# One core, a whole transformer block: the planner charges for a change of TensorE's tiling, PSUM tiles are taken one at a time, and the last expert's second layer goes by column halves

## The chip, the cores and the metric

One core of a Trainium2 chip runs the whole program. The metric is the device time of one execution in microseconds (us), the median of the runs shown.

## What is computed

The input is 256 tokens of width 1024 in float32. Four parts follow one another, each added to the residual `x`:

- **Layer 1**: a norm, one projection of 4896 columns, a forgetting attention (8 heads), a sparse attention (8 heads, three branches), sigmoid gates, and an output projection `w_out`.
- **Mixture of experts**: a norm, a router that gives each token two of 16 experts, and for each expert `silu(t @ w_gate) * (t @ w_up)`, weighted, times `w_down` (1024 to 512 to 1024). 

```python
hid = jax.nn.silu(jnp.einsum('td,edf->etf', t, w_gate)) * jnp.einsum('td,edf->etf', t, w_up)
hid = hid * combine.T.astype(hid.dtype)[:, :, None]
y = jnp.einsum('etf,efd->td', hid, w_down)
```

- **Two hybrid layers**: a norm, a projection to `q, f, i(v), z` of a gated linear recurrence (8 heads of 128) and `q, k, v, z` of a windowed attention (16 heads of 64), and an output projection `w_out_2` of 2048 rows, normed before it is added.

All weights are read from HBM once, some 200 MB.

## The kernel before

**One program order from a planner.** Nothing is ordered by the hardware or by hand. The kernel is written as tasks (Python generators) that yield one operation at a time, and `Sched.run` plays them against a model of the engines: it holds a clock for each engine, gives each yielded operation a ready time, and on the engine that can go first picks the ready task of the lowest priority number (`P_EDGE` -1, `P_SPLIT` 0, `P_EVAC` 1, `P_SIDE` 2, `P_LATE` 3, `P_MAIN` 9). The order picked is the order of the instruction streams. A task can also wait for a flag, for another task, or for a free buffer (`Res`). Every instruction is recorded at line 216 (`go`), so the profile's rows are told apart by tile names.

**Main products and side products.** The tasks of `P_MAIN` issue the large products: weights against activations. Float32 is carried as a high and a low part in fp32r (`hh` and `hl`, halves `w`), three products for one (`mm3`). The weights arrive as 1 MB pieces (`raw`, tasks of `loader`). For layer 1 and the hybrids each piece is split by ScalarE and VectorE into two halves `w` (`K.half_max` limits how many halves are held); the experts' pieces are used as they are ("whole", "pair"). `K.raw_max` limits the pieces held, and `K.slots` (23 buffers) is shared by pieces, halves and activations.

The side tasks (attention, recurrence, evacuations, transposes) put small products between the main ones. Three tilings of TensorE's array occur: full (128 rows by 128 columns), by columns (128x64: the experts' products, the recurrence's `bank<-ha`, attention's second products `bank<-ap,kv`), and by rows (64x128: attention's scores `bank<-kv,qaT`). Two products of a split tiling that lie on different halves run side by side. A plain float32 product shows as two records.

**The experts.** For expert `e` the main task issues the gate and up products (32 records, `bank<-raw,xt`) and then the second layer of the expert before it, `down(e-1)` (16 records, `bank<-raw,route`). Beside it run `rows_of(e)` (transposes and small products that make the placing matrix `P2` and the weights `ws`), `hidden(e)` (ScalarE and VectorE make silu and product, then two transposes to `hT`) and `combine(e)` (scale the result `py`, split it into a high part on 64 partitions and the low part on the other 64, and four products that add it to the PSUM tiles `acc`). All of these are in the full tiling. Before the second expert group, `halves` splits `x` into `xh` and `xl`. After the last expert the edge to the next layer runs: residual, norm, transposes, `hh` and `hl`.

**PSUM.** Four tiles `acc` (`acc_tile`) hold main results, four `bank`s side results. `out_proj` takes four `acc` tiles and then goes over groups of input columns; a group starts when its heads are done. The hybrid's projections go in a written order that ends with `za3`, `z3`; the first group of `out_proj` needs heads 0 and 1, the second heads 2 and 3, the last two the attention pairs.

`keep_warm` puts products of ones (`warm<-ones`) where the planner sees TensorE idle.

Of the kernel before, what the change touches and what calls it, by code (L numbers as in the profile page):

```python
# [82 lines left out]
class Op:  # L83

    __slots__ = ("alts", "ins", "outs", "half", "ready", "banks", "rows")

    def __init__(self, alts, ins, outs, half=(0, 2)):
        self.alts, self.ins, self.outs, self.half, self.ready = alts, ins, outs, half, None
        self.banks = ()

# [41 lines left out]
class Sched:  # L132
# [4 lines left out]
    def __init__(self, nc):  # L137
        self.clk = {"PE": 600.0, "DVE": 600.0, "ACT": 1900.0, "POOL": 600.0, "SP": 600.0}
        self.dma = 0.0
        self.cols = [0.0, 0.0]  # L140
        self.readers = {}
        self.work, self.cold = [], True
        self.fill = self.halfway = None
        self.slot = {}
        self.acc = {}
        self.tasks, self.n = [], 0
        self.made = self.sent = 0
        self.nc = _NC(self, nc)
# [29 lines left out]
    def op(self, eng, op, f, a, k):  # L178
# [43 lines left out]
        if eng == "PE":  # L222
            o.rows = ins[0].shape[0] / 128 * min(1.0, n / 0.6 / cost if op == "matmul" and ins[-1].dtype == F32 else 1.0)
        else:
            o.banks = {self.slot.get(x.tensor.name, x.tensor.name) for x in aps if str(x.space) == "PSUM"}
# [45 lines left out]
    def _product(self, o, start, cost):  # L271
        lo, hi = o.half
        start = max(start, self.clk["PE"])

# [6 lines left out]
        end = max(start + 53, other) if beside else start + cost  # L281
# [49 lines left out]
    def run(self):  # L331
        while self.tasks:
# [16 lines left out]
            for eng, c in self.clk.items():  # L349
                pick = None  # L350
                for t in self.tasks:
                    if t.pend is None:
                        continue
                    for alt in t.pend.alts:
                        if alt[0] == eng:
# [7 lines left out]
                            key = (late, r if late else 0.0, -1 if t is self.halfway and eng == "PE" else t.prio, t.seq)  # L363
# [48 lines left out]
TO_PE, IDLE = 200.0, 150.0  # L412
HOLD = 200
# [4 lines left out]
def setup(ctx, tc, I):  # L418
# [21 lines left out]
    K.slots, K.tinies = Res(SLOTS), Res(TINY)  # L440
    K.raws, K.raw_max, K.halves, K.half_max = 0, 3, 0, 4
# [46 lines left out]

class Unit:
# [22 lines left out]
def loader(K, between):  # L512
# [5 lines left out]
    def load():  # L518
        yield ("if", lambda: K.go)
        for i, u in enumerate(K.plan):  # L520
            yield ("if", lambda: K.raws < K.raw_max and K.slots.free)
            K.raws += 1
            raw, s = yield from big(K, [128, 2048], "raw")
# [11 lines left out]
    def part(u, i, j, src, sh, w, s):  # L535
# [5 lines left out]
        if all(f.done for f in u.flag):  # L541
            K.raws -= 1
            K.slots.release(raws.pop(i)[1])

    sch.spawn(load(), P_SPLIT)
    for i, u in enumerate(K.plan):
        yield wait(loaded[i])
        if u.how in ("whole", "pair"):
# [129 lines left out]
def out_proj(K, key, groups, done, last=1):  # L678
# [3 lines left out]
    ps = []  # L682
    for i in range(4):
        p = yield from acc_tile(K, [128, 512])
        ps.append(p)
# [3 lines left out]
    def go(g, c, j, t):  # L689
        oh, ol = groups[g][1]()  # L690
# [651 lines left out]
def moe(K, edge, done, before):  # L1342
# [105 lines left out]

    class Group:
# [10 lines left out]
    def rows_of(e):  # L1460

        yield wait(t_w, t_rows.get(e - 1), ys.get(e - 2))
        for t in range(2):
            yield nc.vector.tensor_scalar(dup[:, t].rearrange("p (i s) -> p i s", i=2),
                                          K.c("slot")[:, None, :].to_broadcast([128, 2, CAP]), posm[:, t, e:e + 1], None, op0=OP.is_equal)
        p2, b_ = yield from bank(K, [128, 258])
# [10 lines left out]
    def halves():  # L1477
# [3 lines left out]
        for t in range(2):  # L1481
            yield from split(K, *(a[0][:, t].rearrange("p (k d) -> p k d", k=8) for a in xhl), K.x[:, t].rearrange("p (d k) -> p k d", k=8))
# [46 lines left out]
    def hidden(e, pg, b_):  # L1529
# [6 lines left out]
        K.banks.release(b_)  # L1536
        ph, b_ = yield from bank(K, [128, 2, 128])
# [8 lines left out]
    def combine(e, py, b_):  # L1546
# [8 lines left out]
        yield wait([sp(part(c), P_EVAC if e < NE - 1 else P_EDGE) for c in range(2)])  # L1555
        K.banks.release(b_)
        for t in range(2):
            for c in range(2):
                yield nc.tensor.matmul(acc[2 * t + c][0], P2[:, e % 2, t], ty[:, c], start=(e == 0), stop=(e == NE - 1))
                if e == NE - 1:  # L1560
                    done(t, c, acc[2 * t + c])

    hid = {}

    def down(e):
# [10 lines left out]
        ys[e] = sp(combine(e, py, b_), P_EVAC if e < NE - 1 else P_EDGE)  # L1576
# [12 lines left out]
    for e in range(NE):  # L1589
# [4 lines left out]
        t_rows[e] = sp(rows_of(e), P_SIDE)  # L1594
        pg, b_ = yield from bank(K, [128, 2, 256])
        for u_ in range(4):
# [9 lines left out]
            drop_whole(K, u)  # L1606
        if j == 3:
# [3 lines left out]
        hid[e] = sp(hidden(e, pg, b_), P_EVAC)  # L1611
# [26 lines left out]
    yield from down(NE - 1)  # L1638
    yield wait(ys[NE - 1])
# [630 lines left out]
```

## Time and profile before

| | us |
|---|---|
| median of three runs (lowest, highest) | 1006.81 (1002.85, 1007.44) |
| the profiled execution: time, span | 1005.22, 1003.4 |
| TensorE busy, weight loads busy | 975.9, 748.5 |
| VectorE busy, ScalarE busy | 701.4, 496.7 |
| mean granted TensorE clock | 0.996 of full |

The span is from the first to the last instruction; what lies around it is 1.8 us. Matmuls are pipelined, so one that lasts 0.28 us may be followed by the next after 0.12: the step from start to start is the pace. Stages in the span: layer 1 to 250, experts from 250 to 500, the hybrids from 500 to 745 and from 745 on.

### The profile page before, as it was taken

Reading aid. Unit: us, or ns where it says so; the run is one execution under the profiler, and the core shown is the slowest. Engines: PE = TensorE matmul, PEld = TensorE weight load, DVE = VectorE, ACT = ScalarE, POOL = GpSimd, SP = SyncE. Lnnn points to the kernel's source line nnn. Section 1 sums busy time; section 2 is a strip of 40 time slices with the busy share of each in tenths; the row PEclk is TensorE's granted clock in tenths of the full one; section 3 lists DMA queues with packets and bytes.
Section 4 is the critical chain, followed back from the end, with each engine's and each line's share of the span. In section 5 each row is a group of like instructions: output and inputs, shape, how many; then the busy total and the mean of one; then the engine's idle time right before and its main releaser. Section 6 shows DMA issues by size and latency. Waiting matters only on the chain.

```text
span 1003.4 us, 16635 instructions
## 1 busy us (share of the span) xinstructions
PE 975.9 (97%) x6335; PEld 748.5 (75%) x6335; DVE 701.4 (70%) x1755; ACT 496.7 (50%) x1054; POOL 23.2 (2%) x64
## 2 busy tenths in 40 slices
PE   7999999999999999999899999999999999999998
PEld 6877898897434343434588979888888897988887
DVE  5777888685364444545656898999768489899942
ACT  5556679741121111114335658668664365866841
POOL 0101000000000000000000000000000000000000
PEclk9999999999999999999999999999999999999999
DMA  8822593797899999989910224433936232442321
GB/s 299 293 81 85 170 318 113 266 378 269 302 390 388 407 409 409 409 343 391 363 63 1 84 84 128 130 104 120 336 122 218 67 103 86 130 146 102 125 107 42
DMA packets 106578, 210.33 MB, mean 210 GB/s; under 512 B 6174, under 2 KB 54544, under 8 KB 106496
## 3 DMA queue, kind: packets, MB, share of 16 engines
q1 hardware_dynamic: 105248, 206.00, 57.3%
q0 software_dynamic: 1248, 3.22, 1.0%
q8 instruction: 52, 0.85, 0.4%
q14 instruction: 30, 0.25, 0.1%
HBM read 208.16 MB, written 1.05 MB: 208 GB/s over the span
## 4 chain that ended last, share of the span: by engine, by line
PE 46%; DVE 8%; ACT 1%; issue 1%; DVEq 0%
PE acc L216 32%; PE bank L216 12%; DVE ha L216 3%; DVE w L216 2%; PE warm L216 1%; DVE ap L216 1%; ACT ha L216 1%; DVE hb L216 1%; DVE hn L216 0%; DVE rows L216 0%; DVE tiny L216 0%; DVE x L216 0%; DVE og L216 0%; DVE za L216 0%; ACT w L216 0%
## 5 line engine op out<-in xcount | busy, mean ns | idle before, releaser
L216 DVE TENSOR_TENSOR w<-raw,w 128x1024 fp32r<-128x1024 f32 (+1 forms) x196 | 233.2, 1211 | 28.5 <-ACT w L216 27.4
L216 PE MATMUL acc<-hh,w 128*128 128x256 f32 x1280 | 247.4, 289 | 0.0
L216 ACT ACTIVATE w<-raw 128x1024 fp32r<-128x1024 f32 (+1 forms) x196 | 198.7, 1040 | 46.7 <-PE acc L216 26.4
L216 PEld LDWEIGHTS acc<-hh,w 128*128 128x128 f32 x1280 | 202.9, 192 | 6.2 <-issue 4.1
L216 PE MATMUL acc<-hl,w 128*128 128x256 f32 x640 | 184.8, 289 | 0.0
L216 PE MATMUL acc<-w,hh 128*128 128x512 f32 (+2 forms) x512 | 155.5, 380 | 0.2
L216 PEld LDWEIGHTS acc<-hl,w 128*128 128x128 f32 x640 | 122.6, 192 | 2.3 <-issue 0.7
L216 PE MATMUL bank<-raw,xt 128*64 128x512 f32 x512 | 118.1, 599 | 1.2 <-DVE xt L216 1.2
L216 PEld LDWEIGHTS acc<-w,hh 128*128 128x128 f32 x512 | 92.6, 188 | 17.3 <-issue 2.2
L216 PE MATMUL acc<-w,hl 128*128 128x512 f32 (+2 forms) x256 | 96.6, 377 | 0.0
L216 PE MATMUL acc<-w,og 128*128 128x512 f32 x384 | 88.7, 390 | 0.0
L216 PEld LDWEIGHTS acc<-w,og 128*128 128x128 f32 x384 | 71.9, 188 | 14.8
L216 ACT ACTIVATE route<-bank,route 128x256 f32<-128x256 f32 x16 | 7.6, 473 | 144.9 <-PE bank L216 144.9
L216 PEld LDWEIGHTS bank<-raw,xt 128*64 128x64 f32 x512 | 33.6, 136 | 58.5 <-issue 53.0
L216 DVE TENSOR_TENSOR ha<-ha 128x128 f32<-128x128 f32 (+5 forms) x216 | 69.3, 352 | 0.6
L216 ACT ACTIVATE ap<-ap,tiny 128x256 f32<-128x256 f32 (+1 forms) x98 | 42.9, 448 | 49.0 <-DVE tiny L216 36.5
L216 PE MATMUL bank<-raw,route 128*64 128x512 f32 x256 | 60.3, 604 | 0.0
L216 PEld LDWEIGHTS acc<-w,hl 128*128 128x128 f32 x256 | 48.3, 189 | 8.2 <-issue 1.0
L216 PE MATMUL warm<-ones 128*128 128x256 f32 x275 | 40.1, 297 | 4.6 <-ACT ones L437 2.4
L216 PEld LDWEIGHTS warm<-ones 128*128 128x128 f32 x275 | 36.3, 198 | 8.1 <-ACT ones L437 2.4
L216 PEld LDWEIGHTS bank<-raw,route 128*64 128x64 f32 x256 | 17.4, 138 | 31.8 <-issue 29.5
L216 PE MATMUL bank<-ha 128*64 128x96 f32 (+2 forms) x608 | 37.9, 246 | 0.0
(276 smaller groups left out, 1330.3 us busy)
## 6 DMA issues: line engine op xcount, KB each, us to landing
raw<-in_w_in_dram SPq DMA_DIRECT2D x68, 1024.0 KB, 7.5
raw<-in_w_gate_dram SPq DMA_DIRECT2D x64, 512.0 KB, 8.9
raw<-in_w_up_dram SPq DMA_DIRECT2D x64, 512.0 KB, 9.9
raw<-in_w_down_dram SPq DMA_DIRECT2D x32, 1024.0 KB, 11.5
raw<-in_w_out_dram SPq DMA_DIRECT2D x20, 1024.0 KB, 5.2
raw<-in_cmp_k_w_dram SPq DMA_DIRECT2D x2, 1024.0 KB, 5.7
raw<-in_cmp_v_w_dram SPq DMA_DIRECT2D x2, 1024.0 KB, 5.8
raw<-in_w_fox_up_dram SPq DMA_DIRECT2D x2, 1024.0 KB, 12.2
```

What stands on the lines that cost most here:

```text
L216: go = lambda: f(*a, **k)
```

## The change

- **The planner** gets a tiling for each product (`o.mode`) and adds `SWITCH` (95 ns) when it changes. A side product of another tiling than the current one, of priority between `P_EDGE` and `P_MAIN`, is put behind the main products until `GATHER` (1500 ns) after it became ready. Two halves side by side are modelled 2 ns apart, not 53.
- **Experts**: flags `gate[e]`, set when the gate and up products of `e` are issued. `hidden(e)` transposes after `gate[e+1]`, `combine(e)` multiplies after `gate[e+2]`, `rows_of(e)` uses TensorE after `gate[e]`: all three now fall between gate and up of one expert and `down` of the one before. The tasks of the last two experts get `P_EDGE`.
- **The last `down`** becomes `down_last`: all products of columns 0 to 511, then of 512 to 1023; the two array halves hold two partial sums, which are scaled, split and added by eight products instead of four, the first column half while the second is multiplied.
- **`out_proj`** takes an `acc` tile when its first product comes.
- **`loader`** holds at most four pieces that are yet to be split (`K.parts`).
- **`halves`** splits `x` in eight steps instead of two.

```diff
@@ Sched.op
+            o.mode = (ins[0].shape[0] <= 64, aps[0].shape[0] <= 64) if op == "matmul" and ins[-1].dtype == F32 else (False, False)
@@ Sched._product
+        if o.mode != self.mode:
+            self.mode = o.mode
+            start += SWITCH
+            self.clk["PE"] = start
+            self.cols = [max(c, start) for c in self.cols]
-        end = max(start + 53, other) if beside else start + cost
+        end = max(start + 2, other) if beside else start + cost
@@ Sched.run
-                            key = (late, r if late else 0.0, -1 if t is self.halfway and eng == "PE" else t.prio, t.seq)
+                            prio = -1 if t is self.halfway and eng == "PE" else t.prio
+                            if eng == "PE" and t.pend.mode != self.mode and P_EDGE < t.prio < P_MAIN and r < t.pend.ready + GATHER:
+                                prio = P_MAIN + 0.1
+                            key = (late, r if late else 0.0, prio, t.seq)
+SWITCH, GATHER = 95.0, 1500.0
@@ loader
-            yield ("if", lambda: K.raws < K.raw_max and K.slots.free)
+            whole_ = u.how in WHOLE
+            yield ("if", lambda: K.raws < K.raw_max and K.slots.free and (whole_ or K.parts < 4))
             K.raws += 1
+            K.parts += not whole_
@@ out_proj
-    ps = []
-    for i in range(4):
-        p = yield from acc_tile(K, [128, 512])
-        ps.append(p)
+    ps = {}
     def go(g, c, j, t):
+        if 2 * t + c not in ps:
+            ps[2 * t + c] = yield from acc_tile(K, [128, 512])
@@ rows_of
-        yield wait(t_w, t_rows.get(e - 1), ys.get(e - 2))
+        yield wait(t_w, t_rows.get(e - 1))
...
+        yield wait(gate[e] if e else None, ys.get(e - 2))
         p2, b_ = yield from bank(K, [128, 258])
@@ halves
-            yield from split(K, *(a[0][:, t].rearrange("p (k d) -> p k d", k=8) for a in xhl), K.x[:, t].rearrange("p (d k) -> p k d", k=8))
+            for k in range(0, 8, 2):
+                yield from split(K, *(a[0][:, t].rearrange("p (k d) -> p k d", k=8)[:, k:k + 2] for a in xhl),
+                                 K.x[:, t].rearrange("p (d k) -> p k d", k=8)[:, k:k + 2])
@@ hidden
+        yield wait(gate[e + 1] if e < NE - 1 else None)
         ph, b_ = yield from bank(K, [128, 2, 128])
@@ combine
-        yield wait([sp(part(c), P_EVAC if e < NE - 1 else P_EDGE) for c in range(2)])
+        yield wait([sp(part(c), P_EVAC if e < NE - 2 else P_EDGE) for c in range(2)])
         K.banks.release(b_)
+        yield wait(gate[e + 2] if e < NE - 2 else None)
@@ new
+    def combine_last(c, py, b_, ty2):
+        e = NE - 1
+        yield wait(ys.get(e - 1), t_rows[e])
+        w = ws[:, 0, e:e + 1]
+        yield nc.scalar.activation(ty2[:, c, 0], py, AF.Copy, scale=w)
+        yield nc.vector.scalar_tensor_tensor(ty2[:, c, 1], py, w, ty2[:, c, 0].bitcast(F32), op0=OP.mult, op1=OP.subtract)
+        K.banks.release(b_)
+        for i in range(2):
+            for t in range(2):
+                yield nc.tensor.matmul(acc[2 * t + c][0], P2[:, e % 2, t], ty2[:, c, i], start=False, stop=(i == 1))
+                if i:
+                    done(t, c, acc[2 * t + c])
+    def down_last():
...
+        for c in range(2):
+            py, b_ = yield from bank(K, [128, 512])
+            for h, u in enumerate(us):
+                w = yield from whole(K, u)
+                for b in range(2):
+                    yield nc.tensor.matmul(py[64 * b:64 * b + 64], hT[:, e % 2, b, 64 * h:64 * h + 64], w[:, b, 512 * c:512 * c + 512],
+                                           start=(h == 0), stop=(h == 1))
+            cs.append(sp(combine_last(c, py, b_, ty2), P_EDGE))
@@ moe
-        t_rows[e] = sp(rows_of(e), P_SIDE)
+        t_rows[e] = sp(rows_of(e), P_SIDE if e < NE - 2 else P_EDGE)
+        gate[e].done = True
-        hid[e] = sp(hidden(e, pg, b_), P_EVAC)
+        hid[e] = sp(hidden(e, pg, b_), P_EVAC if e < NE - 2 else P_EDGE)
-    yield from down(NE - 1)
-    yield wait(ys[NE - 1])
+    yield from down_last()
```

## Rows read from the trace of the kernel before

**Rows 1.** Stretches: us; PE, PEld, DVE, ACT, POOL busy; clock; DMA share; GB/s.
```profile
555.00:696.70 141.70, 140.00 (x1217) 124.57 (x1217) 130.44 (x362) 95.85 (x198) 3.21 (x7) 1.00 0.33 105
...
480.00:483.40 3.40, 3.40 (x8) 1.10 (x7) 0.29 (x1) 0.00 (x0) 0.00 (x0) 0.50 1.08 363
```

**Rows 2.** PE's timeline, a hybrid: start, us, tiles, array rows*columns, records, [idle <-releaser].
```profile
569.66 0.40 PE L216 MATMUL acc<-hh,w 128*128 128x256 f32 x2
569.99 0.88 PE L216 MATMUL bank<-ha 128*64 128x96 f32 x16
570.80 0.39 PE L216 MATMUL acc<-hl,w 128*128 128x256 f32 x1
571.03 0.40 PE L216 MATMUL acc<-hh,w 128*128 128x256 f32 x2
```

**Rows 3.** PE's timeline, first and last of 31 split-tiled stretches, first hybrid.
```profile
565.23 0.69 PE L216 MATMUL bank<-ha 128*64 128x64 f32 x16
...
693.70 0.86 PE L216 MATMUL bank<-ap,kv 128*64 128x256 f32 x6
```

**Rows 4.** PE's timeline, one expert in the steady stretch.
```profile
446.25 2.80 PE L216 MATMUL bank<-raw,xt 128*64 128x512 f32 x12
448.97 1.19 PE L216 MATMUL acc<-rows 128*128 128x512 f32 x4
...
450.66 4.51 PE L216 MATMUL bank<-raw,xt 128*64 128x512 f32 x20
455.00 3.60 PE L216 MATMUL bank<-raw,route 128*64 128x512 f32 x16
458.53 0.44 PE L216 MATMUL bank<-cp,route 128*128 128x128 f32 x2
458.90 2.79 PE L216 MATMUL bank<-raw,xt 128*64 128x512 f32 x12
```

**Rows 5.** PE's timeline beside `halves`.
```profile
296.00 0.43 PE L216 MATMUL bank<-cp,route 128*128 128x128 f32 x2 [1.46 <-DVE route L216]
```

**Rows 6.** PE's timeline at the end of the last expert.
```profile
467.66 3.60 PE L216 MATMUL bank<-raw,route 128*64 128x512 f32 x16
471.19 3.74 PE L216 MATMUL warm<-ones 128*128 128x256 f32 x29
478.87 0.41 PE L216 MATMUL bank<-cp,route 128*128 128x128 f32 x2 [3.94 <-DVE route L216]
...
479.98 1.98 PE L216 MATMUL bank<-raw,route 128*64 128x512 f32 x4
...
486.19 1.93 PE L216 MATMUL warm<-ones 128*128 128x256 f32 x14
...
489.46 0.98 PE L216 MATMUL acc<-rows 128*128 128x512 f32 x3 [0.47 <-DVE rows L216]
```

**Rows 7.** All engines' timeline: the first hybrid's output projection begins.
```profile
696.75 5.18 PE L216 MATMUL warm<-ones 128*128 128x256 f32 x42
...
702.08 0.74 DVE L216 SCALAR_TENSOR_TENSOR hb<-acc,lbt,hb 128x512 f32<-128x512 f32 x1
...
711.78 0.69 DVE L216 TENSOR_TENSOR og<-hb,og 128x512 fp32r<-128x512 f32 x1 [0.70 <-ACT og L216]
```

**Rows 8.** All engines' timeline: `hidden` of experts 14 and 15, ScalarE and VectorE.
```profile
442.56 0.47 ACT L216 ACTIVATE route<-bank,route 128x256 f32<-128x256 f32 x1 [8.49 <-PE bank L216]
444.30 1.00 DVE L216 SCALAR_TENSOR_TENSOR route<-bank,route 128x256 f32<-128x256 f32 x2 [0.93 <-ACT route L216]
...
469.45 2.01 ACT L216 ACTIVATE w<-raw 128x1024 fp32r<-128x1024 f32 x2 [0.54 <-DMA raw<-in_w_in_dram]
...
471.36 0.46 ACT L216 ACTIVATE route<-bank,route 128x256 f32<-128x256 f32 x1
```

**Rows 9.** Timelines: SP's first piece for the experts, PE's first product on one.
```profile
188.50 0.34 SPq L216 DMA_DIRECT2D raw<-in_w_gate_dram  x1
...
250.31 1.94 PE L216 MATMUL bank<-raw,xt 128*64 128x512 f32 x8 [0.62 <-DVE xt L216]
```

More of the change, by code (lines that the diff above doesn't have):

```diff
@@ L83 @@
 class Op:
-    __slots__ = ("alts", "ins", "outs", "half", "ready", "banks", "rows")
+    __slots__ = ("alts", "ins", "outs", "half", "ready", "banks", "rows", "mode")
     def __init__(self, alts, ins, outs, half=(0, 2)):
@@ L89, in __init__ @@
         self.banks = ()
+        self.mode = None
 class _Eng:
@@ L142, in __init__ @@
         self.work, self.cold = [], True
+        self.mode, self.turned = (False, False), False
         self.fill = self.halfway = None
@@ L440, in setup @@
     K.slots, K.tinies = Res(SLOTS), Res(TINY)
+    K.parts = 0
     K.raws, K.raw_max, K.halves, K.half_max = 0, 3, 0, 4
@@ L486 @@
     done = False
+WHOLE = ("whole", "pair")
 class Unit:
@@ L542, in part @@
             K.raws -= 1
+            K.parts -= 1
             K.slots.release(raws.pop(i)[1])
@@ L547, in loader @@
         yield wait(loaded[i])
-        if u.how in ("whole", "pair"):
+        if u.how in WHOLE:
             u.half = raws.pop(i)
@@ L1447, in moe @@
     groups = {}
+    gate = [Flag() for _ in range(NE)]
     class Group:
@@ L1554, in part @@
             yield nc.vector.scalar_tensor_tensor(ty[o, c], py[r], w, ty[r, c].bitcast(F32), op0=OP.mult, op1=OP.subtract)
-        yield wait([sp(part(c), P_EVAC if e < NE - 1 else P_EDGE) for c in range(2)])
+        yield wait([sp(part(c), P_EVAC if e < NE - 2 else P_EDGE) for c in range(2)])
         K.banks.release(b_)
+        yield wait(gate[e + 2] if e < NE - 2 else None)
         for t in range(2):
             for c in range(2):
-                yield nc.tensor.matmul(acc[2 * t + c][0], P2[:, e % 2, t], ty[:, c], start=(e == 0), stop=(e == NE - 1))
-                if e == NE - 1:
-                    done(t, c, acc[2 * t + c])
-    hid = {}
+                yield nc.tensor.matmul(acc[2 * t + c][0], P2[:, e % 2, t], ty[:, c], start=(e == 0), stop=False)
+    hid = {}
+    def combine_last(c, py, b_, ty2):
[9 more added lines that the diff above has]
+                if i:
+                    done(t, c, acc[2 * t + c])
+    def down_last():
+        e = NE - 1
+        ty2, s_y = yield from big(K, [128, 2, 2, 512], "ty", F32R)
+        yield wait(hid[e])
+        us = [take(K, "d") for _ in range(2)]
+        cs = []
+        for c in range(2):
[5 more added lines that the diff above has]
+                                           start=(h == 0), stop=(h == 1))
+                if c:
+                    drop_whole(K, u)
+            cs.append(sp(combine_last(c, py, b_, ty2), P_EDGE))
+        yield wait(cs)
+        K.slots.release(s_y)
     def down(e):
@@ L1575, in down @@
             drop_whole(K, u)
-        ys[e] = sp(combine(e, py, b_), P_EVAC if e < NE - 1 else P_EDGE)
+        ys[e] = sp(combine(e, py, b_), P_EVAC if e < NE - 2 else P_EDGE)
     def bounds():
```

## The prediction, written before the change was run

> **What bounds the kernel now.** I read the table of stretches first, then PE's timeline, then the waits. In the first hybrid's middle TensorE shows busy for 140.0 of 141.7 us, at full clock, and DMA for a third [rows 1]: so the stage is worth what TensorE's instruction stream is worth, and a gain has to come out of the steps between its starts. Those steps are not all work. The reader should look at where the tiling changes. Two full products start 0.12 apart; from 569.66 two of them would end at 569.90, but the split one starts at 569.99: 0.09 lost. Behind it the first full product starts at 570.80 and the next at 571.03, 0.23 in place of 0.12: 0.11 lost [rows 2]. The timeline shows 31 such visits in the first hybrid (first and last in [rows 3]), about as many in the second, fewer in layer 1.
>
> Among the experts there are two per expert. Records of 128x64 have a pace p and a loss s from entering and leaving: 12p + s = 448.97 - 446.25 = 2.72, and 36p + s = 458.53 - 450.66 = 7.87, so p = 0.2146 and s = 0.145 [rows 4]. With the 0.09 and 0.11 on the full side [rows 2] a visit costs some 0.34. Here the two transposes between 458.53 and 458.90 would take 0.24 at the 0.12 of a full product, so 0.13 is lost on that side, 0.28 in all [rows 4]. I use 0.33 per visit in the hybrids and 0.31 here.
>
> Then three places where TensorE waits: 1.46 us beside `halves` [rows 5], the end of the experts [rows 6], and the start of each hybrid's output projection, filled by products of ones [rows 7].
>
> **The change, part by part.**
>
> *Flags among the experts.* One period is 12.65 us (446.25 to 458.90) with two visits [rows 4]; the flags leave one. Fourteen experts by 0.31 is 4.3; the same ordering where the next groups' rows are gathered may save some four visits more (an estimate from reading that stretch), 1.2. The new wait: `down(e-1)` now stands right behind the transposes to `hT`. From the first transpose to the first product that reads `hT` the last expert took 479.98 - 478.87 = 1.11 us [rows 6]; the transposes are 0.37 of it. The other 0.74 is covered by four products of `combine` and those of `rows_of`, 450.66 - 448.97 = 1.69 together [rows 4]. If the cover were gone, 15 x 0.74 = 11 us. Queued behind `down` is the next gate work, which needs nothing else. `halves` in eight steps takes away TensorE's wait for `dup`: 1.5 [rows 5]. Sum -7; bounds -9 and +4.
>
> *The end of the experts.* Before: the last gate product ends at 467.66, the transposes of `hidden(15)` start at 478.87, 11.2 later [rows 6]. ScalarE began that chain only at 471.36, behind pieces of the next layer at 1 us each [rows 8]. Undisturbed, expert 14's chain runs from 442.56 to 445.30, 2.7 [rows 8]. With `P_EDGE` it goes ahead of the splits, but now starts only when `rows_of(15)` has made `ws`, behind two transposes (0.37) and the 1.69 above, some 2.2, plus 0.6 for the copy: 2.2 + 0.6 + 2.7 + 0.8 (handing over) = 6.3. So 4.9 earlier; `down(14)`, 16 records by 0.2146 = 3.4, lies inside. The wait of 3.94 [rows 6] shrinks to some 1; behind it the clock stood at 1.2 GHz for 3.4 us, from 480.0 to 483.4 [rows 1], where the records take twice the time: 1.7 back, if the shorter wait leaves the clock at 2.4. Last, `combine` of expert 15 in halves: before, 3.3 us lie from the last product (ones follow at 486.19) to the closing `acc` products at 489.46 [rows 6]. After: a ScalarE and a VectorE pass over 128x512, both taken at the 0.74 of [rows 7], and 0.5 for handing over, 2.0: 1.3 saved. Four more `acc` products, 0.9, of which half lies under the second column half. Sum -7; bounds -3 (the clock falls all the same) and -11 (the chain waits for nothing at all, and the norm behind it, which can start on the first column half, gains as well).
>
> *`out_proj`, twice.* The last projection ends at 696.75; 5.18 us of ones follow, until VectorE frees the fourth `acc` tile at 702.08 + 0.74 = 702.82 [rows 7]. Taken one by one, three tiles are free and the first group can start at once: 5.0 less per hybrid at most. What is late next: the second group needs heads 2 and 3, whose `og` is complete at 711.78 + 0.69 = 712.5 [rows 7]. The first group is 48 products of 512 columns; at some 0.23, by the 0.12 of 256 columns [rows 2], that is 11.0 from 696.75, with the heads' own products (an estimate) 2.0 more, 709.7. So 2.8 of the 5.0 is lost again if that chain stays where it is, nothing if it moves up. I take 3 per hybrid. Sum -6; bounds -3 and -10.
>
> *Gathering in the hybrids and layer 1.* Visits come 141.7 / 31 = 4.6 us apart [rows 1, 3], the hold is 1.5, so about a quarter falls together: 8 x 0.33 = 2.6 per hybrid, -5 in all, of which I take -4, because VectorE is busy for 130.4 of the 141.7 [rows 1] and will not follow all of it. Layer 1: -1. Bounds -13 (half of the visits) and 0, and a loss below.
>
> *Few unsplit pieces.* The loads for the experts start at 188.5, 61.8 us before the first product on them [rows 9]. With four pieces allowed, the last two of layer 1's output weights wait for halves to come free, which is when `up` drops them; some 18 us later by an estimate from PE's timeline. 44 us of lead are left: 0. In the first hybrid fewer pieces lie ready, but both hybrids run on three pieces at a time once they have begun (`K.raw_max`), and DMA is busy for a third [rows 1]: 0. Bounds 0 and +5. The planner's 2 ns for 53 changes no work: 0.
>
> Sum: 7 + 7 + 6 + 4 + 1 = 25. The profiled execution took 1005.2 (span 1003.4, and 1.8 around it): 980.2. The median is 1.6 above that execution, so **982**.
>
> One thing speaks against the gathering term. The stretch from 555 shows 124.6 us of weight loads and 130.4 of VectorE in 141.7 [rows 1]. The Trainium skill, "Perfetto Trace Analysis", section "Identifying the Most-Contended Engine", says that matmul busy time doesn't measure TensorE's headroom, that its weight loads' share does, and that the engine with the highest share is the one to work on first. By that rule VectorE comes first there, and taking seams out of TensorE's stream gives nothing in this stage: 987 in place of 982. It is the mechanism of the second rival.
>
> **The rivals.**
>
> 1. *The hold is too short.* Side products come in serial chains; with 1.5 us against 4.6 between visits few meet, and the visits stay near 30. For it: chains of recurrence steps wait on VectorE in between. Against it: several heads and pairs run at once. Hybrids and layer 1 then give 0: 982 + 5 = 987.
> 2. *VectorE bounds the hybrids.* Visits fall, but waits for VectorE take their place, and the heads' chain behind the last projection stays late (out_proj at its bound, -3 in place of -6): 982 + 5 + 3 = 990. For it: 92% busy [rows 1]. Against it: TensorE hardly waits there now.
> 3. *`down` waits for `hT`.* The cover in front of `down` goes first or not at all: +11, 993. Against it: `hidden` is spawned before the others and of higher priority than `rows_of`.
> 4. *Slower: the hold starves VectorE.* Each recurrence product held back lets VectorE stand. It has 141.7 - 130.4 = 11.3 us to spare per hybrid [rows 1]. With some 19 recurrence visits at up to 1.5 us, 28 us would be held, 17 more than it has, 34 in both: 982 + 5 + 34 = 1021. It decides from about 25 us lost per hybrid, 1.3 per visit, and pays only where VectorE has nothing else, as splitting weights, to do. So it is unlikely.
>
> **How the numbers follow.** Forecast 0.60, rivals 0.12, 0.12, 0.08, 0.08. The forecast's own range, with its terms off by about a third together, is 972 to 991. Below it: the edge and projections at their far bounds, 970. Above: rivals 1 to 3 lie inside 993, and the sum with each term at the small end (flags 0, edge -3, projections -3, the rest 0) is 1006.8 - 6 = 1001; I end at 999. So 970 to 999. What a measurement of this kernel can tell from no change is about 0.5%, 5 us. Faster by more than that is everything below 1001.8: the forecast and rivals 1 to 3, but for their tails, 0.86; within it 0.07, mostly their tails; slower 0.07, the fourth rival.
>
> **What would show it.** One visit per expert and a period near 12.3; `hidden(15)`'s transposes some 6 us after the last gate product, with no stretch at half clock; no 5 us of ones ahead of `out_proj`, but perhaps 1 to 3 in front of its second group; some 22 split stretches per hybrid. Wrong would make it: TensorE waiting for `hT` at each expert; VectorE's share falling in the hybrids while the stretch from 555 grows; ones or DMA waits at the first experts.

## The result, and the profile after

The changed kernel takes 982.33 us (median of 4 runs, 979.04 to 983.03) against 1007.12 for the kernel before beside it: a ratio of 0.976, 95% interval 0.972 to 0.979. The forecast was 982, so the sum was met. Several of its terms were not: errors of -6.5 and +5.0 us in them nearly cancelled, and that is luck.

The profiled execution has a span of 980.1 us, 23.3 less. I compared where the same work stands in the two traces, by TensorE's timeline: first and last gate product of the experts, the 25th product of the next layer, the last product of each hybrid's projections, the 49th of each output projection (there its second group begins). Differences of those times, in us, for this kernel and those of the experiments:

| kernel | layer 1 | experts | edge | hybrid 0 | to 49th | hybrid 1 | to 49th | rest | span |
|---|---|---|---|---|---|---|---|---|---|
| before | 250.3 | 216.9 | 38.4 | 191.0 | 17.9 | 231.5 | 17.9 | 39.6 | 1003.4 |
| changed | 250.4 | 212.7 | 29.8 | 187.2 | 15.1 | 227.9 | 17.3 | 39.6 | 980.1 |
| c1 changed again | 249.8 | 212.7 | 29.7 | 187.3 | 15.1 | 228.0 | 17.4 | 39.6 | 979.7 |
| e1 no flags | 250.8 | 214.9 | 28.1 | 187.3 | 15.1 | 227.9 | 15.1 | 39.6 | 978.9 |
| e2 no gathering | 246.8 | 213.0 | 27.1 | 190.4 | 16.2 | 231.0 | 16.2 | 39.6 | 980.4 |
| e3 four tiles | 251.5 | 212.7 | 30.2 | 187.3 | 17.7 | 227.8 | 17.7 | 39.6 | 984.5 |
| e4 any unsplit | 251.0 | 211.9 | 31.0 | 187.3 | 18.9 | 227.9 | 15.1 | 39.6 | 982.7 |
| e5 no edge priority | 251.5 | 212.7 | 34.4 | 187.2 | 15.1 | 227.9 | 15.1 | 39.6 | 983.6 |
| e6 no halves | 250.8 | 212.7 | 30.0 | 187.3 | 17.4 | 227.9 | 15.1 | 39.6 | 980.8 |
| e7 gather late | 246.9 | 214.2 | 29.5 | 187.2 | 17.4 | 227.9 | 18.7 | 39.6 | 981.4 |
| e8 late branch | 250.8 | 208.0 | 29.1 | 187.2 | 15.1 | 228.4 | 18.8 | 39.6 | 977.1 |
| e9 lo on VectorE | 250.5 | 212.0 | 30.1 | 186.7 | 14.6 | 227.3 | 14.6 | 39.7 | 975.6 |
| e10 early heads | 248.9 | 212.5 | 29.5 | 187.8 | 13.1 | 229.8 | 13.1 | 39.6 | 974.2 |
| e11 all | 247.5 | 209.6 | 31.9 | 187.7 | 13.1 | 228.4 | 13.1 | 39.6 | 970.9 |

Such a table is worth more than the medians here, though each row is one execution. The hybrids, where an edit does not touch them, mostly agree within some 0.2 us from kernel to kernel (hybrid 0: 187.2 or 187.3 nine times over), while the times of one kernel scatter by 4. Layer 1 is looser: nine of the kernels (the changed one, c1, e1, e3, e5, e6, e8, e9, e10) have the same order of instructions there and need 248.9 to 251.5. What differs is TensorE's granted clock, which falls to half in a stretch in some executions and not in others. The same stretch of the changed kernel and of e10:

```profile
107.00:119.00 12.00, 9.63 (x69) 9.46 (x68) 9.69 (x19) 7.69 (x14) 0.00 (x0) 0.86 0.44 146
```

```profile
107.00:119.00 12.00, 9.65 (x83) 9.48 (x82) 10.48 (x21) 9.22 (x16) 0.00 (x0) 1.00 0.49 156
```

The clock is 0.86 on average in the first and 1.00 in the second, and behind it the changed kernel is 1.6 us later, with the same instructions. So a difference of up to 2.6 us in layer 1, or of 1.7 in the experts, need not come from an edit.

Stretches of the changed kernel, columns as in [rows 1]:

```profile
540.00:680.00 140.00, 138.30 (x1236) 125.76 (x1236) 130.30 (x363) 95.48 (x197) 4.65 (x8) 1.00 0.34 107
430.20:433.70 3.50, 3.42 (x10) 1.27 (x12) 0.26 (x1) 0.00 (x0) 0.00 (x0) 0.54 1.03 403
```

The first hybrid's middle looks as in [rows 1], though it is shorter by 3.8: busy shares say nothing of seams. Its split-tiled stretches fell from 31 [rows 3] to 24, in the second hybrid too. The second line, half clock among the experts, has no counterpart in the profile before. TensorE's timeline, one expert and the place of the second line:

```profile
423.82 3.65 PE L218 MATMUL bank<-raw,route 128*64 128x512 f32 x16
430.28 4.06 PE L218 MATMUL bank<-raw,xt 128*64 128x512 f32 x10 [2.81 <-DMA raw<-in_w_up_dram]
...
444.36 7.04 PE L218 MATMUL bank<-raw,xt 128*64 128x512 f32 x32
451.32 0.44 PE L218 MATMUL bank<-cp,route 128*128 128x128 f32 x2
...
453.18 3.65 PE L218 MATMUL bank<-raw,route 128*64 128x512 f32 x16
456.67 0.60 PE L218 MATMUL bank<-raw,xt 128*64 128x512 f32 x2
```

One visit per expert, and a period of 456.67 - 444.36 = 12.31 against 12.65 [rows 4], as forecast. But from 427.5 to 430.3 TensorE stands, and behind that ten records take 4.06 at half clock. This is the branch for tokens over capacity (`overflow`, all engines pass it): the weight load of the first product waits for line 1714, which is the branch. The DMA named as releaser brings a piece of a later expert; those of expert 13 had all landed by 416.1. The weight load in the changed kernel, then the products behind the branch in e3, which has the same order of TensorE's and VectorE's instructions among the experts:

```profile
430.25 0.23 PEld L218 LDWEIGHTS bank<-raw,xt 128*64 128x64 f32 x4 [3.66 <-PEq L1714]
```

```profile
433.01 3.23 PE L218 MATMUL bank<-raw,xt 128*64 128x512 f32 x14 [2.91 <-DMA raw<-in_w_up_dram]
```

Before, the same branch cost 1.79, with the full clock behind it. In e3 TensorE stands as long as in the changed kernel and goes on at full clock, fourteen records in 3.23. Of the eleven profiles of changed kernels with the branch in this place, seven have half clock behind it and four (e1, e3, e4, e9) do not. So the standing belongs to the branch, but the half clock behind it comes in some executions only.

The end of the experts, TensorE, then ScalarE:

```profile
465.50 3.65 PE L218 MATMUL bank<-raw,route 128*64 128x512 f32 x16
469.08 1.33 PE L218 MATMUL warm<-ones 128*128 128x256 f32 x9
471.91 0.41 PE L218 MATMUL bank<-cp,route 128*128 128x128 f32 x2 [1.49 <-DVE route L218]
...
473.05 1.08 PE L218 MATMUL bank<-raw,route 128*64 128x512 f32 x4
...
474.95 2.79 PE L218 MATMUL bank<-raw,route 128*64 128x512 f32 x12
477.67 1.66 PE L218 MATMUL acc<-ty,rows 128*128 128x512 f32 x6
...
483.67 0.63 PE L218 MATMUL bank<-cp,hn 128*128 128x128 f32 x4 [0.51 <-DVE hn L218]
```

```profile
465.75 2.01 ACT L218 ACTIVATE w<-raw 128x1024 fp32r<-128x1024 f32 x2 [7.48 <-DMA raw<-in_w_in_dram]
467.78 0.47 ACT L218 ACTIVATE route<-bank,route 128x256 f32<-128x256 f32 x1
468.30 1.06 ACT L218 ACTIVATE w<-raw 128x1024 fp32r<-128x1024 f32 x1
469.26 0.85 ACT L218 ACTIVATE route<-route 128x256 f32<-128x256 f32 x2
```

Against [rows 6] the 3.94 of standing is 1.49 and the clock stays full. The transposes of `hidden(15)` still come 8.8 us after the last gate product (at 463.1), not 6: pieces `w` of the next layer stand ahead of the chain and inside it, priority or no.

The two output projections, TensorE:

```profile
680.23 5.42 PE L218 MATMUL acc<-w,og 128*128 128x512 f32 x23
685.49 1.47 PE L218 MATMUL bank<-hb,V 128*128 128x256 f32 x8
...
691.83 0.50 PE L218 MATMUL bank<-sq,ones 128*128 128x512 f32 x1 [0.50 <-POOL sq L218]
...
693.78 1.59 PE L218 MATMUL warm<-ones 128*128 128x256 f32 x12
695.21 2.02 PE L218 MATMUL acc<-w,og 128*128 128x512 f32 x8
...
937.10 0.50 PE L218 MATMUL bank<-sq,ones 128*128 128x512 f32 x1 [2.75 <-POOL sq L218]
```

The 5.18 of ones ahead of the first group [rows 7] is gone, and ones with a short wait stand ahead of the second, as forecast. In the second hybrid TensorE waits 2.75 for GpSimd where it waits 0.50 in the first. The cause stands in the rows of VectorE, and of GpSimd, at the two places:

```profile
686.02 7.97 DVE L218 TENSOR_TENSOR w<-raw,w 128x1024 fp32r<-128x1024 f32 x6
...
929.03 6.89 DVE L218 TENSOR_TENSOR w<-raw,w 128x1024 fp32r<-128x1024 f32 x6
```

```profile
689.56 2.21 POOL L218 TENSOR_TENSOR sq<-hb,sq 128x512 fp32r<-128x512 f32 x1 [17.69 <-ACT sq L218]
...
932.58 4.46 POOL L218 TENSOR_TENSOR sq<-hb,sq 128x512 fp32r<-128x512 f32 x1 [17.71 <-ACT sq L218]
```

The same GpSimd pass takes 2.21 us beside six VectorE passes that take 7.97, or 4.46 beside six that take 6.89. In the kernel before, VectorE made this pass, in 0.69:

```profile
704.57 0.69 DVE L216 TENSOR_TENSOR sq<-hb,sq 128x512 fp32r<-128x512 f32 x1 [0.61 <-ACT sq L216]
```

The kernel lets the planner choose between the two engines (`either`), and in the new order it chose GpSimd.

### The profile page after: what moved, and what is told of

It is laid out like the page before. It is cut to its first block, busy times and chain, and to the rows that moved or that the text cites. A ratio compares the mean times of both kernels' runs of the same rounds, so it can differ in the third digit from the quotient of the medians.

```text
span 980.1 us, 16442 instructions
## 1 busy us (share of the span) xinstructions
PE 951.6 (97%) x6230; PEld 734.7 (75%) x6230; DVE 688.8 (70%) x1753; ACT 504.4 (51%) x1064; POOL 32.9 (3%) x68
## 4 chain that ended last, share of the span: by engine, by line
PE 64%; DVE 12%; DMA 12%; issue 6%; ACT 3%; SPq 1%; POOL 1%; DVEq 0%; POOLq 0%; ACTq 0%
PE acc L218 42%; PE bank L218 22%; DMA raw<-in_w_up_dram 6%; DVE w L218 3%; DMA raw<-in_w_down_dram 3%; DMA raw<-in_w_in_dram 2%; DVE ha L218 2%; ACT ap L218 1%; DVE ap L218 1%; DVE hb L218 1%; SPq L218 1%; POOL sq L218 1%; DVE tiny L218 1%; DVE rp L218 1%; ACT w L218 1%
## 5 line engine op out<-in xcount | busy, mean ns | idle before, releaser
L218 PE MATMUL bank<-raw,xt 128*64 128x512 f32 x512 | 115.7, 602 | 4.3 <-DMA raw<-in_w_up_dram 2.8
L218 PEld LDWEIGHTS bank<-raw,xt 128*64 128x64 f32 x512 | 36.7, 138 | 74.6 <-issue 64.7
L218 ACT ACTIVATE ap<-ap,tiny 128x256 f32<-128x256 f32 (+1 forms) x94 | 41.6, 451 | 51.7 <-DVE tiny L218 38.4
L218 DVE COPY route<-bank 128x2 f32<-128x2 f32 (+1 forms) x31 | 8.8, 283 | 63.3 <-PE bank L218 63.3
L218 PE MATMUL bank<-ha 128*64 128x96 f32 (+2 forms) x608 | 35.8, 244 | 0.1
L218 PEld LDWEIGHTS bank<-ha 128*64 128x64 f32 (+1 forms) x608 | 30.0, 139 | 4.8 <-issue 0.7
```

The source lines that it names most:

```text
L218: go = lambda: f(*a, **k)
```

## The experiments

Theory: the sum was right by its terms, with the branch and GpSimd's pass as losses that it did not have. The rivals are those of the prediction, and for each surprise of the comparison another. All ratios are to the kernel before on the same chip; two kernels of one group differ surely only where their runs do not overlap, so I read most verdicts from the table.

**e1, no flags.**

```diff
-        yield wait(t_w, t_rows.get(e - 1))
+        yield wait(t_w, t_rows.get(e - 1), ys.get(e - 2))
...
-        yield wait(gate[e] if e else None, ys.get(e - 2))
...
-        yield wait(gate[e + 1] if e < NE - 1 else None)
...
-        yield wait(gate[e + 2] if e < NE - 2 else None)
```

> The changed kernel without the gate flags (rows_of, hidden and combine go when their data are there, rows_of waits for ys at its start as before); gathering, edge, projection as changed. In the instruction order this has 11 more tiling visits among the experts. Theory: each visit is worth 0.31 us, so 3.4 us more than the changed kernel, about 986, with the experts' period going from 12.3 back towards 12.65, and the wait at the branch in front of expert 13 unchanged. Rival A: the flags pay more than their visits, because what they gather also waits less: +6 or more, 988. Rival B: the flags cost what they gain (they are why the clock falls after the branch): 0 or less, 982 or below.

984.09 (980.64 to 986.17), ratio 0.979 (0.978 to 0.981). The experts take 2.2 us longer, the edge 1.6 less. At the branch TensorE stood for 2.03 here, not 2.81, and kept its full clock. Without these two differences, 0.8 and 1.7, the flags give 4.7 for 12 visits (39 split-tiled stretches against 27), somewhat more than the 0.31 of each. Rival B is half right: the flags give part back, 0.8 at the branch, and at the edge, where without `gate[15]` the chain of the last expert starts earlier (transposes 6.1 us after the last gate product, not 8.8; half clock behind them takes 1.6 of that away). That the flags are why the clock falls behind the branch is not borne out: e3, e4 and e9 have the flags and the full clock.

**e2, no gathering.**

```diff
-SWITCH, GATHER = 95.0, 1500.0
+SWITCH, GATHER = 0.0, 0.0
```

> The changed kernel with the planner's price of a tiling change and its hold set to 0; flags, edge, projection as changed. The instruction order has some 8 more visits behind the experts by a coarse count (the traces of the kernels before and after differ by 13), one more among the experts, 2 in layer 1. Theory: a visit is worth 0.33 us on the path, so +3 to +5, 985 to 987. Rival (VectorE sets the pace in the hybrids): the visits come back and the time stays, 982 within 1 us, with TensorE's waits for VectorE shrinking by as much.

982.44 (981.12 to 982.94), ratio 0.977 (0.975 to 0.979). The time is the rival's, the reason is not: each hybrid is longer by 3.1 or 3.2, so that gathering is worth 6.3 there, but layer 1 is 3.6 shorter without it and the edge 2.7. Each hybrid has 31 split-tiled stretches again: seven more by 0.33 are 2.3, and TensorE's waits there are 0.6 and 0.8 longer, which is nearly all of it. Of layer 1's 3.6, 1.6 is the half clock at 113 us, which this profile does not have. At the edge no `w` piece stands in the chain of expert 15, ScalarE's rows first and then TensorE's:

```profile
462.82 0.47 ACT L218 ACTIVATE route<-bank,route 128x256 f32<-128x256 f32 x1 [7.93 <-DVE route L218]
463.65 0.86 ACT L218 ACTIVATE route<-route 128x256 f32<-128x256 f32 x2 [0.36 <-DVE route L218]
```

```profile
465.71 0.44 PE L218 MATMUL bank<-cp,route 128*128 128x128 f32 x2
```

The transposes come 6.0 us after the last gate product (at 459.7), with no wait ahead of them: 5.6 earlier than before, where the prediction had 4.9 for a chain that goes ahead of the splits. From the time alone I would have dropped a term that is there.

**e3, four tiles at the start.**

```diff
     ps = {}
+    for i in range(4):
+        ps[i] = yield from acc_tile(K, [128, 512])
```

> The changed kernel with out_proj taking four PSUM tiles before its first product, as before. Theory from the comparison of the two traces (net 2.8 in the first hybrid, 0.55 in the second): +3.4, 985.7, with 4 to 5 us of ones in front of the first group of each projection and less or none in front of the second. Rival A (the prediction's term): +6, 988. Rival B (the whole 5.0 per hybrid is worth its length): +10, 992.

983.84 (982.24 to 986.38), ratio 0.978 (0.977 to 0.980). TensorE's timeline at the first projection:

```profile
681.79 4.34 PE L218 MATMUL warm<-ones 128*128 128x256 f32 x35
685.97 1.47 PE L218 MATMUL bank<-hb,V 128*128 128x256 f32 x8
```

The ones are back in front, and both projections reach the 49th product after 17.7 us; with tiles one by one that is 15.1 where GpSimd's pass is short. So 2.6 of the 5 is worth anything, 5.2 in both hybrids: the theory for the first, and the prediction's 6, nearly, where GpSimd's pass is short.

**e4, any number of unsplit pieces.**

```diff
-            yield ("if", lambda: K.raws < K.raw_max and K.slots.free and (whole_ or K.parts < 4))
+            yield ("if", lambda: K.raws < K.raw_max and K.slots.free)
```

> The changed kernel without the limit of four unsplit pieces that wait to be split. Theory: loads have tens of us of lead, so 0 within 1.5 us, 982. Rival: the limit keeps VectorE and ScalarE free of splitting at the end of the experts and so makes part of the 10.5 us that the edge became shorter; the instruction order has 8 more products of ones there, +1 to +3, 983 to 985.

982.64 (977.96 to 984.97), ratio 0.976 (0.974 to 0.979): no difference that can be told. The experts are 0.8 shorter; the clock stays full behind the branch here. The edge is 1.3 longer, as the rival has it: 1.1 of it lies between the closing products and the next transposes, where a VectorE pass over weights stands ahead of the residual. VectorE in the changed kernel, then in e4:

```profile
479.80 1.96 DVE L218 TENSOR_TENSOR x<-x,acc 128x512 f32<-128x512 f32 x3
```

```profile
479.79 1.22 DVE L218 TENSOR_TENSOR w<-raw,w 128x1024 fp32r<-128x1024 f32 x1
480.92 1.88 DVE L218 TENSOR_TENSOR x<-x,acc 128x512 f32<-128x512 f32 x3
```

**e5, the priorities of the last two experts as before.**

```diff
-        t_rows[e] = sp(rows_of(e), P_SIDE if e < NE - 2 else P_EDGE)
+        t_rows[e] = sp(rows_of(e), P_SIDE)
...
-        hid[e] = sp(hidden(e, pg, b_), P_EVAC if e < NE - 2 else P_EDGE)
+        hid[e] = sp(hidden(e, pg, b_), P_EVAC)
```

and `P_EVAC` for both steps of `combine`.

> The changed kernel with the priorities of the last two experts as before (rows_of P_SIDE, hidden and combine P_EVAC); the last expert's halves stay. The first comparison found the stretch from the last gate product to the first product of the next layer 10.5 us shorter (32.9 to 22.4) where the prediction had 7. Theory (the prediction's split): the priorities carry 4.9 and the 1.7 of clock, so 6.6 more us than the changed kernel, 989, with the transposes of hidden(15) some 11 us after the last gate product again and a stretch at half clock. Rival: the halves carry most, and the priorities at most 3: 985.

989.47 (984.91 to 993.75), ratio 0.986 (0.983 to 0.988), TensorE's timeline:

```profile
470.18 4.09 PE L218 MATMUL warm<-ones 128*128 128x256 f32 x32
...
479.48 0.44 PE L218 MATMUL bank<-cp,route 128*128 128x128 f32 x2 [0.24 <-DVE route L218]
```

The transposes come 15.3 us after the last gate product, 6.5 later, but `combine` of expert 14 lies in that gap, more ones too, and the clock stays full: the edge is 4.6 longer. Between the theory's 6.6 and the rival's 3. Its median is 6.6 above that of c1; the profiled execution took 985.41, 4 below its median, so the table may understate it.

**e6, the last expert's second layer as before.**

```diff
-    yield from down_last()
+    yield from down(NE - 1)
+    yield wait(ys[NE - 1])
```

and `combine` closes `acc` for it.

> The changed kernel with the last expert's second layer and its combine as before (one PSUM tile, both column halves on the two row halves, four closing products behind it); the priorities of the last two experts stay. Theory (the prediction's split): 0.4 to 1.3 us more, 983. Rival (the halves are where the extra 3.5 us came from, because the norm behind them starts on the first columns): 4 to 5 more, 987. With e5 the two should add up to some 10.5 if they are independent.

985.26 (982.64 to 988.47), ratio 0.982 (0.980 to 0.983). The edge is 0.2 longer, no more, but that is a difference of two. From the last product of `down` to the end of the closing products it takes 4.7 us, against 3.1 in the changed kernel: the halves give 1.5, of which 0.3 is lost again before the next transposes, the theory's large end. And the chain of expert 15 came earlier, its transposes 7.8 us after the last gate product, where the six profiles with the changed kernel's edge have 8.5 to 9.3; whether the edit does that is not shown. The rival is out. The median is higher than all this explains, and its profile, the shortest of its runs, does not say why.

**e7, gathering from the first expert on.**

```diff
-                            if eng == "PE" and t.pend.mode != self.mode and P_EDGE < t.prio < P_MAIN and r < t.pend.ready + GATHER:
+                            if self.gather and eng == "PE" and t.pend.mode != self.mode and P_EDGE < t.prio < P_MAIN and r < t.pend.ready + GATHER:
...
     for e in range(NE):
+        sch.gather = True
```

> The changed kernel with the planner's hold switched on only when the first expert's products are planned, so that it acts among the experts and in the hybrids and not in layer 1. The run without any gathering reached the first expert product 3.6 us earlier and took 3.1 longer in each hybrid. Theory (the hold delays layer 1's attention chain, which its last projection waits for): first expert product at 246.8 in place of 250.4, the hybrids as short as in the changed kernel, 978.5 in all. Rival A: what layer 1 loses comes from the price of a tiling change in the planner, which stays: 982. Rival B: the lead is given back by the loads for the experts, which start no earlier: 981 to 982.

982.47 (978.70 to 984.91), ratio 0.977 (0.975 to 0.979). Layer 1 is 3.4 shorter and the hybrids stay short: the theory of place holds. But 1.6 of the 3.4 is the half clock at 113 us, absent here; against e10, which has the changed kernel's layer 1 without it, 1.9 are left. TensorE's timeline ahead of layer 1's last projection (`no`), of the changed kernel and of this one:

```profile
201.99 0.66 PE L218 MATMUL bank<-nt,te 128*64 128x128 f32 x8
202.57 1.33 PE L218 MATMUL warm<-ones 128*128 128x256 f32 x9
203.74 0.99 PE L218 MATMUL acc<-no,w 128*128 128x256 f32 x7
```

```profile
194.82 0.66 PE L219 MATMUL bank<-nt,te 128*64 128x128 f32 x8
195.41 5.05 PE L219 MATMUL acc<-fo,w 128*128 128x256 f32 x40
200.30 0.88 PE L219 MATMUL acc<-no,w 128*128 128x256 f32 x6
```

Held, the attention chain ends when the other projection has run out, and its own waits; not held, it ends 7 us earlier, 5.6 without the clock, and the other covers it. Yet 1.7 is given back at once, at the first expert. The same eight records of the two kernels:

```profile
250.37 1.94 PE L218 MATMUL bank<-raw,xt 128*64 128x512 f32 x8 [0.62 <-DVE xt L218]
```

```profile
246.94 3.62 PE L219 MATMUL bank<-raw,xt 128*64 128x512 f32 x8 [0.62 <-DVE xt L219]
```

With the same products just ahead of them, a clock of 0.53 stands here in the stretch, 1.00 there. The shorter layer 1 is not what decides it: e3 and e9 have the changed kernel's order up to this place and half clock here as well (in e3 the eight take 3.46). And both projections met the long pass: 2.3 and 1.4 more than in the changed kernel's profile, which ate the rest.

**e8, the branch behind `down(14)`.**

```diff
-            yield from overflow(K, n_max, combF, comb)
-            K.raw_max += 3
+            t_over = sp(overflow(K, n_max, combF, comb, last14), P_EDGE)
...
+    last14.done = True
+    yield wait(t_over)
+    K.raw_max += 3
     K.hold += 1
     yield from down_last()
```

> The changed kernel with the branch for tokens over capacity moved from behind expert 12's products to behind down(14), where TensorE waits for hidden(15) anyway (its three buffers stay taken until then, so that three pieces fewer of the next layer lie ready). Theory: the branch costs 2.8 us of standing and 1.7 us of half clock behind it, and both are hidden at the new place: 4 less, 978, last gate product some 4.5 earlier. Rival A: ScalarE and VectorE pass the branch too, in the chain of hidden(15), so that 1 to 2 us come back at the end: 980. Rival B: the wait there is only moved and now falls into the half clock at the end, or the fewer pieces cost as much: 982 or more.

980.76 (976.07 to 984.67), ratio 0.976 (0.974 to 0.979). TensorE's timeline at the old place and at the new one:

```profile
424.31 3.65 PE L218 MATMUL bank<-raw,route 128*64 128x512 f32 x16
427.79 2.74 PE L218 MATMUL bank<-raw,xt 128*64 128x512 f32 x12
...
465.76 1.30 PE L218 MATMUL warm<-ones 128*128 128x256 f32 x9 [0.88 <-DVEq L1717]
```

The experts are 4.7 shorter, the edge 0.7: 4.96 less in all when the first hybrid's projections end, a little more than the theory's 4.5. Of the 4.7, 1.7 is the half clock behind the branch, which some executions of the changed order do not have either; the rest is about the 2.8 of standing. The wait for `hidden(15)` hides the branch. The second projection's long pass, with half clock behind it, then took 1.5 back.

**c1, the changed kernel again, and e9, `lo` on VectorE.**

```diff
-        yield sch.either(*(e.tensor_tensor(lo, sq, hi.bitcast(F32), op=OP.subtract) for e in (nc.vector, nc.gpsimd)))
+        yield nc.vector.tensor_sub(lo, sq, hi.bitcast(F32))
```

> The changed kernel itself, unaltered, beside the variants of this group. In the eight profiles so far that have its hold and its PSUM tiles one by one, the stretch from the first product of a projection to its 49th took about 15.0 us where GpSimd's late pass sq took 2.21, and 17.2 to 18.8 where it took 4.46, with the same instructions ahead of it. Theory (the pass takes one or the other by chance, from execution to execution): 982 with a spread of some 4 us, each of the two projections at 15.0 or at 17.2 and more. Rival (it depends on the kernel): again 2.21 in the first hybrid and 4.46 in the second.

> The changed kernel with the second part of the heads' squares (lo) always on VectorE, so that GpSimd has no pass in that chain. Theory (GpSimd's pass beside VectorE's six passes over weights makes the second group late by 2.2 to 3.8 us in half of the projections): both projections reach the 49th product after 15.0 us or a little less, 2 to 3 us less than the changed kernel on average, 980, and runs closer together. Rival (VectorE is full there, and lo queues behind the passes over weights, 6.9 us): 17 or more in both, 984.

c1: 982.84 (981.57 to 987.39), ratio 0.979 (0.975 to 0.982). e9: 977.49 (975.40 to 979.26), ratio 0.972 (0.969 to 0.975), all five of its runs below all five of c1. (The expectation counts e2 in, which has no hold; with c1 there are again eight.) Over those eight profiles, 16 projections, the late pass took 2.2 nine times and 4.46 seven times, in either hybrid, in both or in none: 15.1 to the 49th product, or 17.3 and more. e9 has 14.6 in both, with the pass on VectorE, as in the kernel before. That the pass is by chance is seen over kernels; c1 itself repeated the changed kernel's pattern, so the rival is not excluded for one kernel.

**e10, heads that wait for z late** (with e9's edit).

```diff
-    def heads(hp, deps):
+    def heads(hp, deps, z):
...
+        yield wait(z)
         yield nc.vector.tensor_mul(sq, sq, sz)
```

> As e9_lo_vector, and a head no longer waits for its z before its first products, only before its last product with z. In the planned order the second group then has no products of ones ahead of it, and its heads' products stand among the first 12 of the projection in place of the first 36. Theory (the prediction's term: up to 2.8 us per hybrid are lost to heads 2 and 3): 49th product after 12.2 us in both hybrids, as in the run with four tiles behind its ones, so 2.8 + 5.0 = 7.8 less than the profiled run of the changed kernel, some 975. Rival (VectorE's chain ends no earlier): 15 in both, 980.

977.51 (976.03 to 978.25), ratio 0.972 (0.969 to 0.975): no better than e9. The second group has no ones ahead of it and comes after 13.1 us in both; but the head before it is now asked for in the middle of the hybrid, before VectorE has its data. TensorE's timeline there, then the stretch behind it:

```profile
900.60 0.67 PE L218 MATMUL bank<-hb,V 128*128 128x256 f32 x2 [1.36 <-DVE hb L218]
```

```profile
903.60:905.00 1.40, 1.40 (x8) 1.40 (x8) 1.40 (x7) 1.40 (x9) 0.00 (x0) 0.50 0.00 0
```

A wait of 1.36 and half clock behind it: hybrid 1 is 2.5 longer than in e9, hybrid 0 1.1. The 3.0 that the two projections gained went there. The wait comes from the edit, the half clock does not come every time: e11, with the same wait, loses 1.0 and 1.1 and keeps its clock in both.

**e11, all of it**: the edits of e7, e8, e9 and e10 in one kernel.

> The changed kernel with the three edits that gave or should give time: lo on VectorE and z waited for late (as e10_early_heads), the hold from the first expert on (as e7_gather_late), the branch behind down(14) (as e8_late_branch). If they add up: 7 for the projections, 4.7 + 0.7 for the branch, 1.8 to 3.4 for layer 1, some 14 less than the changed kernel, 968. Rival (earlier stages only make later waits longer, as the shorter layer 1 did at the first expert): half of it, 975.

971.46 (969.62 to 975.50), ratio 0.966 (0.962 to 0.970): all five runs below all of c1, 971.46 / 982.84 = 0.988 of it. Between the sum and its half. Layer 1 gives 2.3 and the experts 3.1 of what c1 needs; the edge takes 2.2 back, because the branch now lengthens the last expert's chain (the transposes stand 11.0 us after the last gate product, 8.1 in e8). TensorE at this place:

```profile
466.08 2.26 PE L219 MATMUL warm<-ones 128*128 128x256 f32 x9 [2.90 <-PEq L1719]
468.14 0.63 PE L219 MATMUL bank<-cp,route 128*128 128x128 f32 x2
```

It stands 2.90 at the branch, against 0.88 in e8, and the nine ones behind it run at half clock, 2.26 for 1.30.

## Why the prediction was right, step by step

*Flags and `halves`, 7.* The experts gave 4.2, by the period that was forecast. The step that failed: the sum had no term for the branch, because no edit touched it, and yet it cost 1.0 us more of standing and 1.7 of clock. The longer standing goes with the flags (2.03 without them in e1, 2.97 without gathering in e2); by what way is not shown. The 1.7 is chance, as e3, e4 and e9 show. With those 2.7 the term is 6.9; e8 shows that they are not needed. The third rival (`down` waits for `hT`) is out: no such wait stands in the rows.

*The end of the experts, 7.* Measured 8.6, but not as worked out. To the transposes 11.6 became 8.8: 2.8 for 4.9, since `w` pieces still stand in the chain; in e2, where none does, 11.6 became 6.0. The clock gave 1.6 for 1.7. The closing products came 1.3 sooner behind the last product of `down`, and e6 bears out the halves as the cause. (The sum took off half of the four more products, so 0.85 was left, and put 7.45 at 7.) And 3.0 that were in no term lie between the closing products and the 25th product of the next layer: before, 16 transposes stand ahead of the first product, after, 8. Of the 3.0, e4 gives back 1.1: the limit on unsplit pieces keeps a pass over weights out of the way there. The runs without the priorities, the halves, the flags and gathering all keep the 8 transposes; what brings them is left open. No run took back the eight steps of `halves` or the 2 ns, or two of the other edits at once.

*`out_proj`, 6.* Measured 2.8 and 0.6. The prediction had 5.0 less 2.8 that is lost again if the heads' chain stays, and took 3 per hybrid; 2.8 is what was left in the first. What was missed is that in the new order the chain of heads 2 and 3 hangs on a GpSimd pass with two lengths, where VectorE had made it in 0.69. Where the pass is short, both hybrids give 2.6 to 2.8.

*Gathering, 4 and 1.* In the hybrids 6.3 by e2, above the 4 and inside the bounds. The 4 was cut from 5 because VectorE is busy for 92%; nothing had to be cut. So the second rival falls, and with it the reading that it was taken from: the Trainium skill, "Perfetto Trace Analysis", section "Identifying the Most-Contended Engine", says to work first on the engine with the highest share, and to judge TensorE's headroom by MFU (the reached share of its peak arithmetic rate) and by the share of its weight loads. That put VectorE first; that work on TensorE's stream then gives nothing was the prediction's reading of it. With VectorE as busy as before the stage got shorter by 3.1 per hybrid when seams left TensorE's stream. The measurement decides. In layer 1 the 1 was wrong: holding costs some 1.9 there at equal clock (e7 against e10). Before and changed both have the half clock near 113 us, so that layer 1 did not grow means that something else in the change gave about as much; no run says what.

*Few unsplit pieces, 0.* Right for the loads, by e4's time; the 1.1 at the edge was in no term. The experts' loads began 4 us later, at 192.69 against [rows 9], not 18.

*The slower rival* lost its ground with e2: held products cost VectorE nothing that shows in the hybrids. In layer 1 the hold did starve something, only it was the end of a chain and not VectorE.

So 25 was forecast and 23.3 came in the span: -2.8 (experts), +1.6 (end), -2.6 (projections), +3.4 (the hybrids' 7.4 for 4), -1.1 (layer 1) and -0.2 in rounding and the rest. The mechanisms show in the rows; that their sizes add up to the forecast is luck.

## What to carry to other kernels

Compare stages, not times: e2's time says that gathering does nothing, its stages that it gives 6 in the hybrids while other stages take as much. Look at the granted clock of a stage before a difference is put down to an edit: the same order of instructions took 248.9 or 251.5 us in layer 1. A rule that holds side work back should be switched off where a chain has to end before the main work does. And when work is moved, look at what stands next to it, here a branch that nobody had touched and that cost 1.0 us more of standing.

## What the runs showed of the hardware

A GpSimd pass over 128x512 took 2.21 or 4.46 us beside VectorE's passes over weights (one of the kernel before, at 683.91, took 1.28 beside other work); where it took 2.21, six VectorE passes took 7.97, where 4.46, 6.89. One of the two engines seems to wait for the other, and which one changes.

A branch that all engines pass cost TensorE 1.8 to 3.0 us of standing at its old place, though it isn't taken. After 2.81 of standing ten records took 4.06 (clock 0.54); after 2.91, in e3, fourteen took 3.23 at full clock. So the length of the standing alone does not tell whether the clock falls. The first expert's products ran at 1.00 or 0.53 with the same products ahead of them.
